# Strided attention: TensorE's program as one loop, values copied by quadrants, the block matrix by 0/1 scales

## Chip, cores and metric

The kernel runs on one core of a Trainium2 chip. The metric is the device time of one execution in microseconds; the time before is the median of three runs.

## The reference

```python
batch, heads, seq, dim = (8, 12, 1024, 64)          # stride = 64, float32
scale = 1.0 / np.sqrt(dim)
attend_positions = np.arange(0, seq, stride)        # the same 16 keys for every query
k, v = K[:, :, attend_positions, :], V[:, :, attend_positions, :]
for i in range(seq):
    scores = np.einsum('bhqd,bhkd->bhqk', Q[:, :, i:i + 1, :], k) * scale
    weights = np.exp(scores - np.max(scores, axis=-1, keepdims=True))
    weights = weights / (np.sum(weights, axis=-1, keepdims=True) + 1e-10)
    result[:, :, i, :] = np.einsum('bhqk,bhkd->bhqd', weights, v)[:, :, 0, :]
```

Each of the 96 heads has 1024 queries of 64 numbers, which all attend to the same 16 of its keys and values. Q (25.2 MB) is read and the result (25.2 MB) written once; of K and V 0.4 MB each are used.

## The kernel before

The work is cut into NG = 24 groups of four heads (HG). For each group g, in order:

- `load(g)` (L232): SP issues a DMA of 1 MB of Q into one of 11 buffers `qn`.
- `cast(g)` (L319): POOL turns it to bf16 (`qb`); for the first three groups ACT takes half.
- `transpose(g)` (L331): DVE transposes it within blocks of 32 into `qt`.
- `score_products(g, k)` (L343): 16 matmuls on TensorE with the group's block of `k_t`, which holds the keys of all groups; the scores land in `sc`.
- `largest` (L361), `raise_` (L371), `sums` (L376), `weights` (L383): softmax over 16 keys. DVE takes the maximum, subtracts it, adds up and inverts; ACT takes the exponential; POOL multiplies by the inverse into `wt`.
- `turn_products(g)` (L392): four transpositions on TensorE bring the weights' keys to the partitions (`tp`).
- `spread(g)` (L404): two ACT copies put `tp` into `wb`, one for each half of the partitions, into the columns of that half alone. The rest of `wb` stays zero from a memset, so that `wb` is block diagonal.
- `output_products(g, n)` (L410): eight matmuls of `wb` with the group's value matrix `v_all`, in two halves n, into `o`.
- `evict(g, n)` (L427): ACT copies each half of `o` to one of eight buffers `out_sb`; it waits for the store of eight groups before.
- `queue(g)` and `store` (L489, L452): SP issues the store of two groups (2 MB) and further loads. SP works its list in order, so a store that waits for its data holds up the loads behind it.

The values need preparation. `value_rows(n)` (L294) has TensorE multiply all values with a permutation matrix `perm_v` (built by POOL from the identity) to repeat their rows where the groups need them, and ACT copies the products to `v_rep`. `values(g)` (L311) then has POOL multiply a group's rows with a 0/1 `mask`, into one of two tiles `v_all`.

`Program` (L43) records operations with what they read and write, and derives the semaphore waits. The order of work of each engine is the order of recording: a prologue (L458 to L479), then for each step i the stages of `ORDER` (L526), each with its lag, so that "turn3" at step i is the turn of group i - 3. Operations of TensorE that are marked `looped` are not written out: `pe_stream` (L532) writes one loop of two groups a turn, with waits on four counters (`turned`, `weighted`, `free0`, `free1`), which it lowers again at each turn's end. `scores(0)`, `scores(1)` and the value products come ahead of that loop, written out: 36 matmuls. The loop has (NG + 2) / 2 = 13 turns, and past the last group its stages run on data that nobody uses. For ACT, DVE and POOL all instructions are written out.

Of the kernel before, what the change touches and what calls it, by code (L numbers as in the profile page):

```python
# [168 lines left out]
def kernel(  # L169
# [32 lines left out]
    k_raw = sb.tile([P, NC, D], FP32, name="k_raw")  # L202
# [3 lines left out]
    k_bf = sb.tile([P, NC, D], BF16, name="k_bf")  # L206
    k_r = sb.tile([P, NC, D], BF16, name="k_r")
    v_bf = sb.tile([P, NC, D], BF16, name="v_bf")
    v_rep = sb.tile([P, NC, 2, D], BF16, name="v_rep")
    identity = sb.tile([P, P], BF16, name="identity")  # L210
    perm_v = sb.tile([P, 2, 2, 2, 2, NK], BF16, name="perm_v")
    s_sel = sb.tile([P, 4], BF16, name="s_sel")
    mask = sb.tile([P, 4, D], BF16, name="mask")
    k_t = sb.tile([P, NG + 4, 2, 4 * NK], BF16, name="k_t")
    v_all = [sb.tile([P, 4, D], BF16, name=f"v_all{i}") for i in range(2)]
# [5 lines left out]
    wt = [sb.tile([P, 32, NK], BF16, name=f"wt{i}") for i in range(2)]  # L221
# [34 lines left out]
    id_v = identity.rearrange("p (c b a k) -> p c b a k", c=2, b=2, a=2)  # L256
    for c in range(2):
        for a in range(2):
            op("POOL", lambda c=c, a=a: nc.gpsimd.tensor_copy(
                out=perm_v[:, c, a],  # L260
                in_=id_v[:, c, :, a].unsqueeze(1).to_broadcast([P, 2, 2, NK]),
            ), reads=["identity"], writes=[f"perm{c}{a}"])
    op("POOL", lambda: nc.gpsimd.memset(k_t, 0.0),  # L263
       writes=[f"k_t{c}{s}" for c in range(2) for s in range(4)])
# [8 lines left out]
    op("POOL", lambda: nc.gpsimd.memset(wb_all, 0.0),  # L273
       writes=[f"wb{i}{a}" for i in range(2) for a in range(2)])
# [8 lines left out]
    def keys(c, h, engine):  # L283
        src, dst = 32 * (2 * c + h // 2), 32 * h
        col = 32 * (h % 2) + NK * (h // 2)
        fn = {"DVE": nc.vector.tensor_copy, "ACT": nc.scalar.copy}[engine]
        op(engine, lambda: fn(  # L287
            k_t[dst : dst + 32, c : NG : 2, :, col : col + NK],
            k_r[src : src + 32].rearrange(
                "p n (a k f) -> p a n f k", a=2, f=2  # L290
            )[:, h % 2],
        ), reads=["k_r"], writes=[f"k_t{c}{h}"])

    def value_rows(n):  # L294
# [12 lines left out]
        op("ACT", lambda: nc.scalar.copy(  # L307
            v_rep[:, 6 * n : 6 * n + 6].rearrange("p n c d -> p c n d"), rows
        ), reads=[f"o{n}"], writes=[f"v_rep{n}"])

    def values(g):  # L311
        op("POOL", lambda: nc.gpsimd.tensor_tensor(  # L312
            out=v_all[g % 2], in0=mask,
            in1=v_rep[:, g // 2, g % 2].unsqueeze(1).to_broadcast([P, 4, D]), op=ALU.mult,
        ), reads=["mask", f"v_rep{g // 12}"], writes=[f"v{g % 2}"])
# [3 lines left out]
    def cast(g, shared):  # L319
# [6 lines left out]
        else:  # L326
            op("POOL", lambda: nc.gpsimd.tensor_copy(out=b, in_=q),  # L327
               reads=[f"qn{g % QBUFS}{h}" for h in range(2)],
               writes=[f"qb{g % 2}{h}" for h in range(2)])

# [12 lines left out]
    def score_products(g, k):  # L343
        for i in range(8):
            for f in range(2):
                r = nc.tensor.matmul(  # L346
                    _ap_with(
                        sc_ps[g % 2], [sc_ps[g % 2].ap[0], [64, 2], [1, 32]],
                        extra_offset=128 * (i // 2) + 32 * (i % 2),
                    ),  # L350
# [5 lines left out]
    def scores(g, looped):  # L356
        op("PE", None if looped else lambda: score_products(g, g),
           reads=[f"qt{g % 2}"] + [f"k_t{g % 2}{h}" for h in range(4)],
           writes=[f"sc{g % 2}"], gates=[("turned", g + 1)], looped=looped)
# [23 lines left out]
    def weights(g):  # L383
# [6 lines left out]
        ), reads=[f"ex{g % 2}", f"rec{g % 2}"], writes=[f"wt{g % 2}"], gate="weighted")  # L390
# [9 lines left out]
    def turn(g, looped):  # L400
        op("PE", None if looped else lambda: turn_products(g),
           reads=[f"wt{g % 2}", "identity"], writes=[f"tp{g % 2}{a}" for a in range(2)], gates=[("weighted", g + 1)], looped=looped)

    def spread(g):  # L404
        for a in range(2):
            rows = slice(64 * a, 64 * a + 64)
            op("ACT", lambda rows=rows: nc.scalar.copy(wb[g % 2][rows, :, rows], tp_ps[g % 2][rows]),  # L407
               reads=[f"tp{g % 2}{a}"], writes=[f"wb{g % 2}{a}"])

    def output_products(g, n):  # L410
# [177 lines left out]
```

## Time and profile before

| what | value |
|---|---|
| median of three runs | 128.34 us (128.32 to 128.53) |
| the profiled execution's own time | 129.04 us |
| its span, first to last instruction | 127.3 us |
| DMA: data moved, mean rate over the span | 51.18 MB, 402 GB/s |
| busiest compute engine | ACT, 96.3 us (76%) |
| TensorE's granted clock, mean | 0.844 |

The times of the profile are microseconds from the span's start. PE is TensorE's matmul, PEld its weight load; DVE, ACT, POOL and SP are VectorE, ScalarE, GpSimd and SyncE. A row of a group of instructions names line, engine, operation, written and read tiles, shapes and count, then the busy time in us, the mean of one in ns, and the idle time before them with what ended it. A row by stage gives from and to in us, the stage's length, the busy time of each compute engine, TensorE's granted clock, the mean busy share of the 16 DMA engines, and the GB/s moved. The rate in a short stage counts a packet where it starts, so shares can pass 1. A row of a DMA queue gives its packets, its MB and the time they took as a share of 16 engines over the stretch asked for.

### The profile page before, as it was taken

How to read it: one execution, taken by the hardware profiler on the slowest of the kernel's cores; microseconds unless marked ns; L12 is line 12 of the kernel's file. 1: busy time of each engine (PE TensorE's matmuls, PEld its weight loads, DVE VectorE, ACT ScalarE, POOL GpSimd, SP SyncE). 2: the span in 40 equal slices, each digit the busy share in tenths (PEclk: the TensorE clock that was granted, in tenths of full speed). 3: DMA queues.
4: the chain of work that ended last, by engine and by line, in shares of the span. 5: the costliest groups of instructions: out<-in, count | busy, mean ns of one | idle time of the engine just before them, and what ended most of it. 6: DMA issues, size and time to landing. Idle time of an engine off the chain costs nothing. (4 is left out here: it accounts for less than half of the span.)

```text
span 127.3 us, 2174 instructions
## 1 busy us (share of the span) xinstructions
PE 66.8 (52%) x764; PEld 47.6 (37%) x764; DVE 83.3 (65%) x126; ACT 96.3 (76%) x136; POOL 88.9 (70%) x88
## 2 busy tenths in 40 slices
PE   0003385684656766575555584274666765595000
PEld 0002353562434544352433372262454544383000
DVE  0105977999999999999999995893794665000000
ACT  4299763599999999999999976965974999983000
POOL 5993388999999999999998992893895344400000
PEclk9999999599997799999999958975555699959555
DMA  2998999989999998998999999999999999999980
GB/s 53 408 422 371 484 391 433 474 366 474 422 402 371 448 469 361 427 469 376 443 448 391 417 469 397 422 453 407 404 438 435 412 422 427 438 412 438 402 363 28
DMA packets 6134, 51.18 MB, mean 402 GB/s; under 512 B 3696, under 2 KB 3696, under 8 KB 3696
## 3 DMA queue, kind: packets, MB, share of 16 engines
q1 hardware_dynamic: 6128, 51.12, 96.2%
q14 instruction: 5, 0.04, 0.1%
q8 instruction: 1, 0.02, 0.0%
HBM read 25.95 MB, written 25.17 MB: 402 GB/s over the span
## 5 line engine op out<-in xcount | busy, mean ns | idle before, releaser
L432 ACT COPY out_sb<-o 128x1024 f32<-128x1024 f32 x48 | 46.4, 1015 | 8.3 <-DMA out_dram<-out_sb 6.1
L327 POOL CAST qb<-qn 128x2048 bf16<-128x2048 f32 x21 | 39.7, 1892 | 6.0 <-DMA qn<-in_Q_dram 6.0
L413 PE MATMUL o<-v_all,wb_all 128*128 128x256 bf16 x208 | 36.3, 318 | 3.0 <-ACT out_sb L432 2.9
L346 PE MATMUL sc<-k_t,qt 128*128 (+1 forms) x448 | 24.0, 213 | 20.2 <-DVE qt L338 15.4
L338 DVE STREAM_TRANSPOSE qt<-qb 128x1024 int32<-128x1024 int32 x24 | 29.7, 1239 | 5.0 <-ACT qb L322 3.6
L387 POOL TENSOR_TENSOR wt<-ex,rec 128x512 bf16<-128x512 f32 x24 | 25.4, 1060 | 9.3 <-DVE rec L380 8.6
L346 PEld LDWEIGHTS sc<-k_t,qt 128*128 128x128 bf16 x448 | 21.1, 111 | 26.6 <-DVE qt L338 13.9
L407 ACT COPY wb_all<-tp 64x512 bf16<-64x512 bf16 x48 | 27.7, 577 | 1.4 <-PE tp L394 1.0
L394 PE MATMUL tp<-identity,wt 128*128 128x128 bf16 x104 | 11.9, 246 | 26.4 <-POOL wt L387 26.4
L413 PEld LDWEIGHTS o<-v_all,wb_all 128*128 128x128 bf16 x208 | 20.5, 112 | 12.1 <-ACT out_sb L432 7.7
L377 DVE TENSOR_REDUCE total<-ex 128x32 f32<-128x512 f32 x24 | 16.3, 681 | 11.0 <-ACT ex L372 9.6
L372 ACT ACTIVATE ex<-low 128x512 f32<-128x512 f32 x24 | 15.4, 642 | 4.5 <-DVE low L367 4.5
L394 PEld LDWEIGHTS tp<-identity,wt 128*128 128x128 bf16 x104 | 6.9, 108 | 29.3 <-POOL wt L387 29.3
L367 DVE TENSOR_TENSOR low<-sc,top 128x512 f32<-128x512 f32 x24 | 16.6, 692 | 0.8
L312 POOL TENSOR_TENSOR v_all<-mask,v_rep 128x256 bf16<-128x256 bf16 x24 | 16.1, 670 | 0.5 <-ACT v_rep L307 0.5
L364 DVE TENSOR_REDUCE top<-sc 128x32 f32<-128x512 f32 x24 | 15.2, 632 | 1.1 <-PE sc L346 1.1
L380 DVE RECIPROCAL rec<-total 128x32 f32<-128x32 f32 x24 | 8.5, 353 | 0.8
L324 POOL CAST qb<-qn 128x1024 bf16<-128x1024 f32 x3 | 3.1, 1041 | 3.6 <-DMA qn<-in_Q_dram 3.6
L287 ACT COPY k_t<-k_r 32x384 bf16<-32x384 bf16 x8 | 4.1, 509 | 0.7 <-DVE k_r L278 0.6
L322 ACT CAST qb<-qn 128x1024 bf16<-128x1024 f32 x3 | 3.1, 1045 | 0.0
L263 POOL MEMSET k_t<- 128x3584 bf16 x1 | 3.1, 3085 | 0.0
L278 DVE STREAM_TRANSPOSE k_r<-k_bf 128x384 int32<-128x384 int32 x1 | 0.6, 579 | 3.5 <-ACT k_bf L277 3.5
(19 smaller groups left out, 11.2 us busy)
## 6 DMA issues: line engine op xcount, KB each, us to landing
qn<-in_Q_dram SPq DMA_DIRECT2D x24, 1024.0 KB, 21.4
out_dram<-out_sb SPq DMA_DIRECT2D x11, 2048.0 KB, 21.5
out_dram<-out_sb SPq DMA_DIRECT2D x2, 1024.0 KB, 10.3
k_raw<-in_K_dram SPq DMA_DIRECT2D x1, 384.0 KB, 4.1
v_raw<-in_V_dram SPq DMA_DIRECT2D x1, 384.0 KB, 6.6
```

The costliest lines, as they stand in the source:

```text
L312: op("POOL", lambda: nc.gpsimd.tensor_tensor(out=v_all[g % 2], in0=mask, in1=v_rep[:, g // 2, g % 2].unsqueeze(1).to_broadcast([P, 4, D]), ...
L327: op("POOL", lambda: nc.gpsimd.tensor_copy(out=b, in_=q), reads=[f"qn{g % QBUFS}{h}" for h in range(2)], writes=[f"qb{g % 2}{h}" for h in ...
L338: op("DVE", lambda: nc.vector.transpose(_ap_with(words, [words.ap[0], [1, 2], [D, 16], [2, 32]]), qb[g % 2].bitcast(I32),), reads=[f"qb{g ...
L346: r = nc.tensor.matmul(_ap_with(sc_ps[g % 2], [sc_ps[g % 2].ap[0], [64, 2], [1, 32]], extra_offset=128 * (i // 2) + 32 * (i % 2),), lhsT=_ ...
L367: op("DVE", lambda: nc.vector.tensor_tensor(out=low, in0=s, in1=m.unsqueeze(2).to_broadcast([P, 32, NK]), op=ALU.subtract,), reads=[f"sc{g ...
L372: op("ACT", lambda: nc.scalar.activation(out=ex[g % 2], in_=low, func=AF.Exp, bias=0.0, scale=scale,), reads=["low"], writes=[f"ex{g % 2}"])
L377: op("DVE", lambda: nc.vector.tensor_reduce(out=total[g % 2], in_=ex[g % 2], op=ALU.add, axis=mybir.AxisListType.X,), reads=[f"ex{g % 2}"] ...
L387: op("POOL", lambda: nc.gpsimd.tensor_tensor(out=wt[g % 2], in0=ex[g % 2], in1=rec[g % 2].unsqueeze(2).to_broadcast([P, 32, NK]), op=ALU.mult,
L394: r = nc.tensor.transpose(tp_ps[g % 2][:, 2 * c : 2 * c + 2].rearrange("p a b -> p (a b)"), wt[g % 2][:, 8 * c : 8 * c + 8].rearrange("p t ...
L407: op("ACT", lambda rows=rows: nc.scalar.copy(wb[g % 2][rows, :, rows], tp_ps[g % 2][rows]), reads=[f"tp{g % 2}{a}"], writes=[f"wb{g % 2}{a}"])
L413: r = nc.tensor.matmul(_ap_with(o_ps, [o_ps.ap[0], [128, 2], [256, 2], [1, D]], extra_offset=512 * c + D * u,), lhsT=wb[g % 2][:, 2 * c + ...
L432: op("ACT", lambda: nc.scalar.copy(to[:, half], o_ps[:, half].rearrange("p c (b x) -> p c b x", b=2)), reads=[f"o{n}"] + ready, writes=[f" ...
```

## The change

TensorE's written-out products go. The loop begins with the first scores and has 14 turns; in its first two steps the stages after the scores run on zeros (`idle`), for which `pe_stream` raises three counters beforehand and three tiles are set to zero. The matmuls of the scores write 64 adjacent columns, since the keys' columns in `k_t` now follow the order of the heads.

The values are no longer permuted by TensorE, repeated or masked. One tile `v_all` holds the value matrices of all groups; POOL sets it to zero and copies blocks of 32 partitions of `v_raw` into it, 24 copies spread over the first steps, by `VALUES`: eight for groups 0 to 3 at step 2, then two a step for four steps and one a step for eight. Each copy is recorded as reading what the POOL operation before it wrote (`apart`).

The block matrix `wb` is written by two ACT activations of all 128 partitions, each with a scale of 0 or 1 for each partition (`sel`), in place of two copies of 64 partitions. The memsets of `k_t` and `wb_all` move from POOL to DVE. The keys' raw tiles share memory with the last output buffer.

```diff
-    k_raw = sb.tile([P, NC, D], FP32, name="k_raw")
+    late = out_all[-1].rearrange("p n b x d -> p (n b x d)")
+    k_raw = late[:, 0 : NC * D].rearrange("p (n d) -> p n d", d=D)
+    k_half = late[:, NC * D : 2 * NC * D].bitcast(BF16).rearrange("p (a n d) -> p a n d", a=2, d=D)
+    k_bf, k_r = [k_half[:, i] for i in range(2)]
...
-    k_bf = sb.tile([P, NC, D], BF16, name="k_bf")
-    k_r = sb.tile([P, NC, D], BF16, name="k_r")
-    v_bf = sb.tile([P, NC, D], BF16, name="v_bf")
-    v_rep = sb.tile([P, NC, 2, D], BF16, name="v_rep")
...
-    perm_v = sb.tile([P, 2, 2, 2, 2, NK], BF16, name="perm_v")
-    s_sel = sb.tile([P, 4], BF16, name="s_sel")
-    mask = sb.tile([P, 4, D], BF16, name="mask")
+    sel = sb.tile([P, 2], FP32, name="sel")
...
-    v_all = [sb.tile([P, 4, D], BF16, name=f"v_all{i}") for i in range(2)]
+    v_all = sb.tile([P, NG + 4, 4, D], BF16, name="v_all")
...
-    wt = [sb.tile([P, 32, NK], BF16, name=f"wt{i}") for i in range(2)]
+    wt_all = sb.tile([P, 2, 32, NK], BF16, name="wt_all")
+    wt = [wt_all[:, i] for i in range(2)]
...
-    id_v = identity.rearrange("p (c b a k) -> p c b a k", c=2, b=2, a=2)
-    for c in range(2):
-        for a in range(2):
-            op("POOL", lambda c=c, a=a: nc.gpsimd.tensor_copy(
-                out=perm_v[:, c, a],
-                in_=id_v[:, c, :, a].unsqueeze(1).to_broadcast([P, 2, 2, NK]),
-            ), reads=["identity"], writes=[f"perm{c}{a}"])
-    op("POOL", lambda: nc.gpsimd.memset(k_t, 0.0),
+    op("DVE", lambda: nc.vector.memset(k_t, 0.0),
        writes=[f"k_t{c}{s}" for c in range(2) for s in range(4)])
-    op("POOL", lambda: nc.gpsimd.memset(v_all[1], 0.0), writes=["v1"])
+    op("DVE", lambda: nc.vector.memset(wt_all, 0.0), writes=["wt0", "wt1"])
+    op("DVE", lambda: nc.vector.memset(wb_all, 0.0),
+       writes=[f"wb{i}{a}" for i in range(2) for a in range(2)])
     op("DVE", lambda: nc.vector.tensor_reduce(
-        out=s_sel, in_=identity.rearrange("p (h s k) -> p s h k", h=2, s=4),
+        out=sel, in_=identity.rearrange("p (q h k) -> p h q k", h=2, k=NK),
         op=ALU.max, axis=mybir.AxisListType.XY,
-    ), reads=["identity"], writes=["s_sel"])
-    op("POOL", lambda: nc.gpsimd.tensor_copy(
-        out=mask, in_=s_sel.unsqueeze(2).to_broadcast([P, 4, D])
-    ), reads=["s_sel"], writes=["mask"])
-    op("POOL", lambda: nc.gpsimd.memset(wb_all, 0.0),
-       writes=[f"wb{i}{a}" for i in range(2) for a in range(2)])
+    ), reads=["identity"], writes=["sel"])
+    op("POOL", lambda: nc.gpsimd.memset(v_all, 0.0),
+       writes=[f"v{c}{a}{b}{m}" for c in range(2) for a in range(2) for b in range(2) for m in range(3)] + ["none"])
...
-        col = 32 * (h % 2) + NK * (h // 2)
+        col = NK * h
...
-    def value_rows(n):
-        rows = o_ps[:, 2 * n : 2 * n + 2, 0 : NC // 2 * D].rearrange("p c (n d) -> p c n d", d=D)
-
-        def products():
-            for c in range(2):
-                r = nc.tensor.matmul(
-                    rows[:, c], lhsT=perm_v[:, c].rearrange("p a i b k -> p (a i b k)"),
-                    rhs=v_bf[:, 6 * n : 6 * n + 6], start=True, stop=True,
-                )
-            return r
-
-        op("PE", products, reads=["v_bf"] + [f"perm{c}{a}" for c in range(2) for a in range(2)],
-           writes=[f"o{n}"])
-        op("ACT", lambda: nc.scalar.copy(
-            v_rep[:, 6 * n : 6 * n + 6].rearrange("p n c d -> p c n d"), rows
-        ), reads=[f"o{n}"], writes=[f"v_rep{n}"])
-
-    def values(g):
-        op("POOL", lambda: nc.gpsimd.tensor_tensor(
-            out=v_all[g % 2], in0=mask,
-            in1=v_rep[:, g // 2, g % 2].unsqueeze(1).to_broadcast([P, 4, D]), op=ALU.mult,
-        ), reads=["mask", f"v_rep{g // 12}"], writes=[f"v{g % 2}"])
+    parts = (slice(0, 2), slice(2, 7), slice(7, NC))
+
+    apart = []
+
+    def values(c, a, b, m):
+        src, dst, part = 32 * (2 * c + b), 32 * (2 * a + b), parts[m]
+        op("POOL", lambda: nc.gpsimd.tensor_copy(
+            out=v_all[dst : dst + 32, 3 + c + 2 * part.start : 3 + c + 2 * part.stop - 1 : 2, 2 * a + b],
+            in_=v_raw[src : src + 32, part],
+        ), reads=["v_raw"] + apart, writes=[f"v{c}{a}{b}{m}"])
+        apart[:] = [f"v{c}{a}{b}{m}"]
...
-               reads=[f"qn{g % QBUFS}{h}" for h in range(2)],
+               reads=[f"qn{g % QBUFS}{h}" for h in range(2)] + apart,
                writes=[f"qb{g % 2}{h}" for h in range(2)])
+            apart[:] = [f"qb{g % 2}0"]
...
-                    _ap_with(
-                        sc_ps[g % 2], [sc_ps[g % 2].ap[0], [64, 2], [1, 32]],
-                        extra_offset=128 * (i // 2) + 32 * (i % 2),
-                    ),
+                    sc_ps[g % 2][:, 64 * i : 64 * i + 64],
...
-        ), reads=[f"ex{g % 2}", f"rec{g % 2}"], writes=[f"wt{g % 2}"], gate="weighted")
+        ), reads=[f"ex{g % 2}", f"rec{g % 2}"] + [k for k in apart if k[0] == "v"], writes=[f"wt{g % 2}"], gate="weighted")
...
-    def turn(g, looped):
-        op("PE", None if looped else lambda: turn_products(g),
-           reads=[f"wt{g % 2}", "identity"], writes=[f"tp{g % 2}{a}" for a in range(2)], gates=[("weighted", g + 1)], looped=looped)
+    def turn(g):
+        op("PE", None, reads=[f"wt{g % 2}", "identity"], writes=[f"tp{g % 2}"],
+           gates=[("weighted", g + 1)] if g >= 0 else [], looped=True)
...
-            rows = slice(64 * a, 64 * a + 64)
-            op("ACT", lambda rows=rows: nc.scalar.copy(wb[g % 2][rows, :, rows], tp_ps[g % 2][rows]),
-               reads=[f"tp{g % 2}{a}"], writes=[f"wb{g % 2}{a}"])
-
-    def output_products(g, n):
+            op("ACT", lambda a=a: nc.scalar.activation(
+                out=wb[g % 2][:, :, 64 * a : 64 * a + 64], in_=tp_ps[g % 2],
+                func=AF.Copy, scale=sel[:, a : a + 1],
+            ), reads=[f"tp{g % 2}", "sel"], writes=[f"wb{g % 2}{a}"])
+
+    def output_products(g, k, n):
...
-                    rhs=v_all[g % 2].rearrange("p s d -> p (s d)"), start=True, stop=True,
+                    rhs=v_all[:, k].rearrange("p s d -> p (s d)"), start=True, stop=True,
...
-        op("PE", None, reads=[f"wb{g % 2}0", f"wb{g % 2}1", f"v{g % 2}"], writes=[f"o{n}"],
-           gates=[(f"free{n}", g + 2)], looped=True)
+        op("PE", None, reads=[f"wb{g % 2}0", f"wb{g % 2}1"] + [
+               f"v{g % 2}{a}{b}{int(g >= 4) + int(g >= 14)}" if 0 <= g < NG else "none" for a in range(2) for b in range(2)
+           ], writes=[f"o{n}"], gates=[(f"free{n}", g + 1)] if g >= 0 else [], looped=True)
...
-        ), reads=[f"o{n}"] + ready, writes=[f"out{g % OBUFS}.{n}"],
+        ), reads=[f"o{n}"] + ready, writes=[f"out{g % OBUFS}.{n}"] + ["k_raw", "k_bf", "k_r"] * (g == OBUFS - RUN and not n),
...
+    def idle(i):
+        scores(i)
+        turn(i - 2)
+        for n in range(2):
+            outputs(i - 3, n)
+
...
-    scores(0, False)
     cast(1, True)
+    idle(0)
     largest(0)
     raise_(0)
     transpose(1)
-    scores(1, False)
-    op("ACT", lambda: nc.scalar.copy(v_bf, v_raw), reads=["v_raw"], writes=["v_bf"])
+    idle(1)
     cast(2, True)
     sums(0)
     weights(0)
-    value_rows(0)
-    values(0)
-    value_rows(1)
-    for n in range(2):
-        free([f"v_rep{n}"], n)
...
+    quadrants = [[(c, a, b, m) for c in range(2) for a in range(2) for b in range(2)] for m in range(3)]
+    VALUES = {0: quadrants[0]}
+    VALUES.update((i + 1, quadrants[1][2 * i : 2 * i + 2]) for i in range(4))
+    VALUES.update((i + 5, quadrants[2][i : i + 1]) for i in range(8))
...
-    turns = (NG + 2) // TURN
+    turns = (NG + 4) // TURN
...
+        elif stage == "values" and g in VALUES:
+            for q in VALUES[g]:
+                values(*q)
...
-    ORDER = "transpose0 cast-1 turn3 spread3 sums2 outA4 largest1 evA4 outB4 evB4 values3 scores0 weights2 raise_1 queue4".split()
+    stages = dict(sums=sums, largest=largest, raise_=raise_, queue=queue)
+    ORDER = "transpose0 cast-1 values2 turn3 spread3 sums2 outA4 largest1 evA4 outB4 evB4 scores0 weights2 raise_1 queue4".split()
...
+        pe.sem_inc(gates["weighted"], 2)
+        for n in range(2):
+            pe.sem_inc(gates[f"free{n}"], 3)
         with pe.Fori(0, turns) as turn_:
             for j in range(TURN):
-                pe.wait_ge(gates["turned"], j + 3)
-                score_products(j, turn_ * TURN + (j + 2)).then_inc(done, 1)
+                i = turn_ * TURN + j
+                pe.wait_ge(gates["turned"], j + 1)
+                score_products(j, i).then_inc(done, 1)
                 pe.wait_ge(gates["weighted"], j + 1)
                 turn_products(j).then_inc(done, 1)
                 for n in range(2):
                     pe.wait_ge(gates[f"free{n}"], j + 1)
-                    output_products(j + 1, n).then_inc(done, 1)
+                    output_products(j + 1, i, n).then_inc(done, 1)
```

More of the change, by code (lines that the diff above doesn't have):

```diff
@@ L354, in score_products, with scores @@
         return r
[L356 to L359, printed above, removed]
+    def scores(g):
+        op("PE", None, reads=[f"qt{g % 2}"] + [f"k_t{g % 2}{h}" for h in range(4)],
+           writes=[f"sc{g % 2}"], gates=[("turned", g + 1)], looped=True)
     def largest(g):
@@ L474 @@
     weights(0)
-    value_rows(0)
-    values(0)
-    value_rows(1)
-    for n in range(2):
-        free([f"v_rep{n}"], n)
     early = dict(
         cast=(0, 1, 2), transpose=(0, 1), scores=(0, 1), largest=(0,), raise_=(0,), sums=(0,),
-        weights=(0,), values=(0,),
+        weights=(0,),
     )
+    quadrants = [[(c, a, b, m) for c in range(2) for a in range(2) for b in range(2)] for m in range(3)]
+    VALUES = {0: quadrants[0]}
+    VALUES.update((i + 1, quadrants[1][2 * i : 2 * i + 2]) for i in range(4))
+    VALUES.update((i + 5, quadrants[2][i : i + 1]) for i in range(8))
     DEPTH = 4
-    turns = (NG + 2) // TURN
+    turns = (NG + 4) // TURN
     ahead = 1
@@ L505, in at @@
         elif stage == "scores" and 0 <= g < NG + 4:
-            scores(g, True)
+            scores(g)
         elif stage == "weights" and 0 <= g < NG + 2:
@@ L509, in at @@
         elif stage == "turn" and 0 <= g < NG + 2:
-            turn(g, True)
+            turn(g)
         elif stage in ("outA", "outB") and -1 <= g < NG + 1:
@@ L516, in at @@
             n = int(stage == "evB")
-            free([f"o{n}"] + ["wb00", "wb01"] * (1 - n), n)
+            free(["wb00", "wb01"], n)
         elif stage in ("evA", "evB") and 0 <= g < NG:
@@ L521, in at @@
             cast(g, False)
+        elif stage == "values" and g in VALUES:
+            for q in VALUES[g]:
+                values(*q)
         elif 0 <= g < NG and stage in stages:
             stages[stage](g)
-    stages = dict(sums=sums, largest=largest, raise_=raise_, queue=queue, values=values)
-    ORDER = "transpose0 cast-1 turn3 spread3 sums2 outA4 largest1 evA4 outB4 evB4 values3 scores0 weights2 raise_1 queue4".split()
+    stages = dict(sums=sums, largest=largest, raise_=raise_, queue=queue)
+    ORDER = "transpose0 cast-1 values2 turn3 spread3 sums2 outA4 largest1 evA4 outB4 evB4 scores0 weights2 raise_1 queue4".split()
     for i in range(1, NG + 5):
```

## The prediction

> **What bounds the kernel now.** I read the page first, for the share of each engine and of the DMA.
>
> ```profile
> span 127.3 us, 2174 instructions
> ...
> PE 66.8 (52%) x764; PEld 47.6 (37%) x764; DVE 83.3 (65%) x126; ACT 96.3 (76%) x136; POOL 88.9 (70%) x88
> ...
> DMA  2998999989999998998999999999999999999980
> ...
> q1 hardware_dynamic: 6128, 51.12, 96.2%
> q14 instruction: 5, 0.04, 0.1%
> q8 instruction: 1, 0.02, 0.0%
> ```
>
> No compute engine is busy for more than 76% of the span, while the 16 DMA engines are busy for 96.2% of it with the data queue alone. The chain of waits follows instructions alone; it ends with TensorE's last matmuls, before the last transfer lands, and does not help here. I asked for busy time by stage instead.
>
> ```profile
> core 0: us, PE busy (x) PEld busy (x) DVE busy (x) ACT busy (x) POOL busy (x), PEclk, DMA share, GB/s
> 39.00:40.00 1.00, 0.62 (x12) 0.59 (x13) 0.96 (x3) 0.90 (x3) 0.93 (x3) 0.83 0.35 147
> 40.00:94.00 54.00, 32.44 (x378) 22.81 (x376) 47.29 (x69) 47.88 (x69) 47.42 (x41) 0.85 1.00 425
> 115.00:123.00 8.00, 1.30 (x13) 0.69 (x10) 0.00 (x0) 0.62 (x1) 0.00 (x0) 0.70 0.99 417
> 123.00:124.00 1.00, 0.00 (x0) 0.00 (x0) 0.00 (x0) 0.00 (x0) 0.00 (x0) 0.50 0.53 221
> 124.00:125.00 1.00, 0.00 (x0) 0.00 (x0) 0.00 (x0) 0.00 (x0) 0.00 (x0) 0.50 0.20 82
> 125.00:126.00 1.00, 0.00 (x0) 0.00 (x0) 0.00 (x0) 0.00 (x0) 0.00 (x0) 0.50 0.08 33
> ...
> 125.00:125.25 0.25, 0.00 (x0) 0.00 (x0) 0.00 (x0) 0.00 (x0) 0.00 (x0) 0.50 0.16 66
> 125.25:125.50 0.25, 0.00 (x0) 0.00 (x0) 0.00 (x0) 0.00 (x0) 0.00 (x0) 0.50 0.08 33
> 125.50:125.75 0.25, 0.00 (x0) 0.00 (x0) 0.00 (x0) 0.00 (x0) 0.00 (x0) 0.50 0.08 33
> ```
>
> By the slices of the page and the DMA share of the stages (next to last column) the queue is full from the third microsecond to 123 us, near 1.00; compute starts, idles and ends under it. So a shorter computation buys nothing, and a slower one costs nothing while the queue stays full. What is left is the tail: at 123 us the rate falls from 417 to 221, then 82, then 33 GB/s. All 16 engines give 425, so one gives 26.6. After 124 us two or three work, after 125.25 us one alone. The kernel waits for its slowest DMA engine, about 2 us after most of the others (123.5 to 125.6).
>
> Why is one late? The page lists six packets that are not data but instructions, one of them on a queue of its own (q8). I narrowed the DMA view until it held that packet: the stretch from 27.5 to 29 us.
>
> ```profile
> q8 instruction: 1, 0.02, 4.2%
> ```
>
> 4.2% of 16 engines in 1.5 us is 1.0 us of one engine (0.042 x 16 x 1.5). An engine that never runs dry cannot make that up: 1.0 us of foreign work at 28 us is still there at 125 us. The trace doesn't name the engine, nor whose instructions these are; that it is the engine that ends last is my reading, since 1.0 us is half of its lateness and no other packet is near that size (the five on q14 hold 0.04 MB together).
>
> **The change part by part.** *TensorE's program.* The 32 score matmuls and 4 value matmuls ahead of the loop go; the loop takes 14 turns in place of 13 and runs 784 matmuls (56 x 14) against 764 and a few lost records. Each matmul has a weight load, so the written program loses 72 of its some 210 instructions. I expect the late instruction block to go with them: TensorE is the engine whose program shrinks by a third, and the packet comes early in the loop's second turn.
>
> ```profile
> 18.76 1.25 PE L413 MATMUL o<-v_all,wb_all 128*128 128x256 bf16 x8
> ...
> 25.44 0.89 PE L346 MATMUL sc<-k_t,qt 128*128 x16
> ```
>
> The second turn's scores begin at 25.44 us, the packet lies 2 us later, and the code past the unlooped part is what has been reached for the first time. [...]
>
> Price: at most 1.0 us by the packet's row, if nobody else were late; below, the next engine decides. From 125.00 to 125.25 two packets of 8 KB start (66 GB/s x 0.25 us = 16 KB), later one per quarter, the last at 125.50 to 125.75. So the second-latest engine starts its last packet some 0.5 us (0.25 to 0.75) before the latest. I take **-0.6 us**, nearer to the second engine's distance than to the packet's 1.0, as it limits first. The other bound is 0: no other row shortens the data. The two passes of the loop that compute nothing yet (outputs of 1.25 us by the row above, turns of half as many matmuls) run while TensorE waits for the second group's queries; if that cover were gone, the second scores would start up to 2 us late, well under the slack that the first store has (below).
>
> *Values and memsets.* POOL loses 24 multiplies, four permutation copies and two memsets; it gains one larger memset and 24 quadrant copies (8 of 128, 16 of 320 elements a partition), each behind a wait for the one before.
>
> ```profile
> L327 POOL CAST qb<-qn 128x2048 bf16<-128x2048 f32 x21 | 39.7, 1892 | 6.0 <-DMA qn<-in_Q_dram 6.0
> L387 POOL TENSOR_TENSOR wt<-ex,rec 128x512 bf16<-128x512 f32 x24 | 25.4, 1060 | 9.3 <-DVE rec L380 8.6
> L312 POOL TENSOR_TENSOR v_all<-mask,v_rep 128x256 bf16<-128x256 bf16 x24 | 16.1, 670 | 0.5 <-ACT v_rep L307 0.5
> L263 POOL MEMSET k_t<- 128x3584 bf16 x1 | 3.1, 3085 | 0.0
> L273 POOL MEMSET wb_all<- 128x2048 bf16 x1 | 1.8, 1805 | 0.0
> L259 POOL COPY perm_v<-identity 128x64 bf16<-128x64 bf16 x4 | 0.8, 238 | 0.1
> ...
> L252 POOL TENSOR_SCALAR_AFFINE_SELECT identity<-identity 128x128 bf16<-128x128 bf16 x1 | 0.3, 295 | 0.2 <-POOL identity L251 0.2
> ```
>
> The memset of 7168 elements is 6.2 us (3085/3584 x 7168), about as long as what goes from the same place (3.1 + 1.8 + 0.8 and two smaller ones). So the first cast begins where it did. A cast costs 0.92 ns an element, so a small copy 0.12 + 0.1 = 0.22 us and a larger 0.40; a wait for the engine's own last result 0.24 us (the 0.2 of L252). Bounds: 0.24 (the 64-element copy) to 0.67 (the multiply). The eight first copies take 8 x (0.22 + 0.24) = 3.7 us in place of one multiply of 0.67 and stand ahead of the cast of group 4 and the weights of group 1: POOL is some 3 us late there. Then come two copies a group for four groups: 1.89 + 1.06 + 2 x 0.64 + 0.24 = 4.5 us against 3.62 now. Who waits: the weights, TensorE, ACT's evictions, and behind them on SP the first store and the loads after it.
>
> ```profile
> 31.45 0.63 SPq L34 DMA_DIRECT2D out_dram<-out_sb  x1
> ...
> 116.78 0.54 SPq L34 DMA_DIRECT2D out_dram<-out_sb  x1
> ...
> out_dram<-out_sb SPq DMA_DIRECT2D x1, 1024.0 KB, 9.7
> ```
>
> The first store is issued at 31.45 us, but its bytes move only when the loads before it are through, at the dip at 39 to 40 us (0.35 above): some 6 us of cover after an issue's lead of 1 to 2. Three microseconds late costs **0**. After that a pair of groups needs 4 MB of DMA, 10 us, against 9 us of POOL at its worst, so the cover grows.
>
> *Block matrix by scales.* Two ACT instructions a group stay, of 128 instead of 64 partitions and the same 512 elements each, now activations with a scale.
>
> ```profile
> L407 ACT COPY wb_all<-tp 64x512 bf16<-64x512 bf16 x48 | 27.7, 577 | 1.4 <-PE tp L394 1.0
> L372 ACT ACTIVATE ex<-low 128x512 f32<-128x512 f32 x24 | 15.4, 642 | 4.5 <-DVE low L367 4.5
> L432 ACT COPY out_sb<-o 128x1024 f32<-128x1024 f32 x48 | 46.4, 1015 | 8.3 <-DMA out_dram<-out_sb 6.1
> ```
>
> Between 577 ns and the 642 of the activation: 0 to 0.13 us a group, 0.8 us over the last six groups. ACT waits for stores in between (6.1 us), so earlier lateness is absorbed. [...] Cost 0. The three memsets on DVE (3328 words) take 3.5 to 5 us at 1 to 1.5 ns a word, ready by 5 to 6.5 us; at worst the keys are 0.5 us late, under the same cover.
>
> **Sum** against the profiled execution: its own time 129.04 us is 1.7 over its span; the median of the runs is 128.34. 129.04 - 0.6 = 128.4 profiled, and 128.34 - 0.6 = **127.7 us** for the median.
>
> **Rivals.** *(1) The block is fetched all the same,* by the loop's back branch or because it is another engine's, or it is not the engine that ends last: 128.3 us. For it: the trace names no owner, and the loop branches back before and after. Against: one packet in 13 turns, so branches alone don't bring it. *(2) The first store comes too late.* It decides if the eight copies and what follows cost over 6 us more than now: from 0.9 us a copy, wait included, over twice my estimate. Then every microsecond beyond is lost: at 1.1 us a copy it is 8 x 1.1 - 0.7 = 8.1, 2 us over, and 128.34 - 0.6 + 2 = 129.7 us. Against: no POOL row of that size costs it. *(3) Another engine gets a block instead.* POOL's written program grows by 15 instructions, semaphore waits above all; a packet of 8 KB at the small blocks' price of 0.3 us (the rate of one engine, 26.6 GB/s) falls on one DMA engine. On the one that ends last, with the old block still there: 128.65 us.
>
> **How the numbers follow.** Forecast (block gone, 127.0 to 128.0) 0.60; rival 1 0.22; rival 2 0.07; rival 3 0.11. The range leaves out rival 2 and a gain beyond all of the packet: 126.9 to 128.65; the forecast's own is 126.9 to 128.0. Its low end is 1.4 us of gain: the last engine is done at some 125.6 us, all but three at some 124.2 (82 GB/s is three engines), and the other late ones may be freed too, since the smaller blocks change as well. Some 0.2% (0.26 us) is what a measurement tells from no change. Faster: 0.60 and a little of rival 1, 0.62; same 0.20; slower 0.18.
>
> **What would show it.** No q8 packet between the start and 60 us, a rate that falls from 400 GB/s to nothing within 2 us, and a span near 126.7: right. A q8 packet that is there still, or the same 2.5 us of tail without it: the step on the block is wrong. A DMA share well under 0.9 for over a microsecond around 35 to 45 us: rival 2. POOL's copies should show 0.2 and 0.4 us, the scaled activations 0.58 to 0.65, the first store 32 to 36 us.

## The result, and the profile after

The changed kernel takes 129.05 us (median of 15 runs, 128.28 to 129.53), the kernel before 128.53 us beside it (15 runs, 128.32 to 128.70): ratio 1.0038, 95% interval 1.0022 to 1.0054. It is slower by some 0.5 us, where 0.6 us of gain was forecast.

The page of the changed kernel, the same lines as before:

```profile
span 127.1 us, 2269 instructions
...
PE 67.3 (53%) x784; PEld 49.9 (39%) x784; DVE 86.2 (68%) x129; ACT 97.0 (76%) x133; POOL 83.3 (66%) x81
...
DMA  1999999999898999999999999999999999999990
...
q1 hardware_dynamic: 6128, 51.12, 96.1%
q14 instruction: 5, 0.04, 0.1%
```

The line of q8 is missing: the packet of 16 KB that the kernel before has there (1638 GB/s over the 10 ns from 27.69 us, in which it is the only packet) is gone, as forecast. DMA is as full as it was (96.1% in q1 against 96.2%), and the span 0.2 us shorter in this one execution. Now the end by stages (from, to, length, the engines' busy times, granted clock, DMA share, GB/s):

```profile
123.00:124.00 1.00, 0.00 (x0) 0.00 (x0) 0.00 (x0) 0.00 (x0) 0.00 (x0) 0.50 0.67 279
124.00:125.00 1.00, 0.00 (x0) 0.00 (x0) 0.00 (x0) 0.00 (x0) 0.00 (x0) 0.50 0.14 57
125.00:126.00 1.00, 0.00 (x0) 0.00 (x0) 0.00 (x0) 0.00 (x0) 0.00 (x0) 0.50 0.04 16
...
125.25:125.50 0.25, 0.00 (x0) 0.00 (x0) 0.00 (x0) 0.00 (x0) 0.00 (x0) 0.50 0.00 0
125.50:125.75 0.25, 0.00 (x0) 0.00 (x0) 0.00 (x0) 0.00 (x0) 0.00 (x0) 0.50 0.08 33
```

Less is left after 124 us (57 and 16 GB/s against 82 and 33), so fewer engines are late in this execution; a second profile of the same kernel (e1) has 131 and 16. And one engine still starts its last packet of 8 KB between 125.50 and 125.75 us, as late as in the kernel before. The tail did not grow shorter.

The span is not the whole time. Each run gives its time and its span; the rest lies before the first and after the last instruction. For the changed kernel it is 2.05 us (median of 15), and for the kernel before 1.77 us (35 runs beside the first experiments). The DMA view of the changed kernel, asked for 127 to 130 us, past the span's end:

```profile
DMA packets 1, 0.01 MB, mean 3 GB/s; under 512 B 0, under 2 KB 0, under 8 KB 0
...
q14 instruction: 1, 0.01, 1.1%
```

One packet of instructions of 8 KB comes there (109 GB/s in one slice of 0.075 us), some 1.6 us after the span's end; the same stretch of the kernel before has no packet at all. This is the second half of the answer: some 0.28 us are lost outside the span. The other 0.24 us of this first comparison stay unexplained: the spans of the kernel before are not on record here, and the repetition below (e1) finds 0.26 us outside the span and 0.05 in it.

What was costed at nothing, in the groups of the changed kernel (line, engine, operation, tiles, shapes, count, busy us, mean ns of one, idle time before) and in SP's list (the changed kernel's first two stores):

```profile
L290 POOL CAST v_all<-v_raw 32x320 bf16<-32x320 f32 x16 | 7.2, 447 | 1.0
L263 POOL MEMSET v_all<- 128x7168 bf16 x1 | 6.1, 6072 | 0.0
...
L290 POOL CAST v_all<-v_raw 32x128 bf16<-32x128 f32 x8 | 2.3, 287 | 0.5
```

```profile
L382 ACT ACTIVATE wb_all<-tp,sel 128x512 bf16<-128x512 bf16 x48 | 30.4, 692 | 4.7 <-PE tp L370 4.5
```

```profile
34.28 0.63 SPq L34 DMA_DIRECT2D out_dram<-out_sb  x1
...
42.40 0.59 SPq L34 DMA_DIRECT2D out_dram<-out_sb  x1
```

The copies take 0.29 and 0.45 us, the memset 6.1. The activations take 692 ns each, above the forecast's 642, but overlap (30.4 us / 48 = 0.63 apart). The first store is issued 2.8 us later (34.28 against 31.45). None of it shows in the DMA line.

### The profile page after: what moved, and what is told of

Its sections match the earlier page's. It is cut to its first block, busy times and chain, and to the rows that moved or that the text cites. A ratio compares the mean times of both kernels' runs of the same rounds, so it can differ in the third digit from the quotient of the medians.

```text
span 127.1 us, 2269 instructions
## 1 busy us (share of the span) xinstructions
PE 67.3 (53%) x784; PEld 49.9 (39%) x784; DVE 86.2 (68%) x129; ACT 97.0 (76%) x133; POOL 83.3 (66%) x81
## 3 DMA queue, kind: packets, MB, share of 16 engines
q1 hardware_dynamic: 6128, 51.12, 96.1%
## 5 line engine op out<-in xcount | busy, mean ns | idle before, releaser
L390 PE MATMUL o<-v_all,wb_all 128*128 x224 | 38.6, 317 | 2.5 <-ACT out_sb L410 0.9
L363 POOL TENSOR_TENSOR wt_all<-ex,rec 128x512 bf16<-128x512 f32 x24 | 25.4, 1057 | 17.6 <-DVE rec L356 16.3
L382 ACT ACTIVATE wb_all<-tp,sel 128x512 bf16<-128x512 bf16 x48 | 30.4, 692 | 4.7 <-PE tp L370 4.5
L326 PE MATMUL sc<-k_t,qt 128*128 x448 | 24.0, 213 | 15.8 <-DVE qt L318 11.9
L370 PE MATMUL tp<-identity,wt_all 128*128 128x128 bf16 x112 | 13.0, 249 | 29.8 <-POOL wt_all L363 28.1
L390 PEld LDWEIGHTS o<-v_all,wb_all 128*128 128x128 bf16 x224 | 22.9, 113 | 10.9 <-ACT out_sb L410 3.9
L370 PEld LDWEIGHTS tp<-identity,wt_all 128*128 128x128 bf16 x112 | 7.6, 109 | 32.8 <-POOL wt_all L363 31.0
L290 POOL CAST v_all<-v_raw 32x320 bf16<-32x320 f32 (+1 forms) x24 | 9.5, 394 | 1.5
L263 POOL MEMSET v_all<- 128x7168 bf16 x1 | 6.1, 6072 | 0.0
L277 ACT COPY k_t<-out_sb 32x384 bf16<-32x384 bf16 x8 | 4.1, 508 | 0.7 <-DVE out_sb L268 0.6
```

Of the source, the lines that this page charges most:

```text
L326: r = nc.tensor.matmul(sc_ps[g % 2][:, 64 * i : 64 * i + 64], lhsT=_ap_with(qt[g % 2], [qt[g % 2].ap[0], [2, P]], extra_offset=2 * P * i + f),
L363: op("POOL", lambda: nc.gpsimd.tensor_tensor(out=wt[g % 2], in0=ex[g % 2], in1=rec[g % 2].unsqueeze(2).to_broadcast([P, 32, NK]), op=ALU.mult,
L370: r = nc.tensor.transpose(tp_ps[g % 2][:, 2 * c : 2 * c + 2].rearrange("p a b -> p (a b)"), wt[g % 2][:, 8 * c : 8 * c + 8].rearrange("p t ...
L382: op("ACT", lambda a=a: nc.scalar.activation(out=wb[g % 2][:, :, 64 * a : 64 * a + 64], in_=tp_ps[g % 2], func=AF.Copy, scale=sel[:, a : a ...
L390: r = nc.tensor.matmul(_ap_with(o_ps, [o_ps.ap[0], [128, 2], [256, 2], [1, D]], extra_offset=512 * c + D * u,), lhsT=wb[g % 2][:, 2 * c + ...
```

## The experiments

All were timed in several rounds, each beside the kernel before on the same chip. There were four series, on four chips: e1 to e4, e5 to e8, e9 to e11, and e12. The kernel before had a median span of 127.10, 127.10, 127.05 and 127.00 us in them, so medians of different series can be set side by side to about 0.1 us. Each of e1 to e12 ran 12 times (e10 six times). The table gives the median time, the median span and the median of time less span, in us; POOL and TensorE are the instructions written in their programs, a matmul with its weight load counted as two.

| kernel | TensorE | POOL | time | span | over the span | ratio to before (95%) |
|---|---|---|---|---|---|---|
| before (with e1 to e4) | 209 | 124 | 128.87 | 127.10 | 1.77 | |
| e1 changed, again | 142 | 139 | 129.17 | 127.15 | 2.03 | 1.0024 (1.0010 to 1.0037) |
| e2 changed, TensorE long | 209 | 139 | 129.19 | 127.15 | 2.03 | 1.0026 (1.0013 to 1.0039) |
| e3 before, POOL long | 209 | 140 | 129.09 | 127.05 | 2.03 | 1.0011 (0.9997 to 1.0026) |
| e4 changed, POOL short | 142 | 106 | 128.79 | 127.00 | 1.78 | 0.9982 (0.9967 to 0.9997) |
| e5 before, POOL 132 | 209 | 132 | 128.94 | 127.15 | 1.81 | 1.0008 (0.9990 to 1.0026) |
| e6 e4, 1 score matmul | 78 | 106 | 128.13 | 126.30 | 1.84 | 0.9940 (0.9921 to 0.9958) |
| e7 e4, stored in reverse | 142 | 106 | 128.71 | 126.90 | 1.79 | 0.9987 (0.9968 to 1.0006) |
| e8 e4 again | 142 | 106 | 128.78 | 127.00 | 1.79 | 0.9992 (0.9975 to 1.0010) |
| e9 e6 + 15 tiny matmuls | 138 | 106 | 128.62 | 126.85 | 1.77 | 0.9990 (0.9979 to 1.0001) |
| e10 e6 + 7 tiny matmuls | 106 | 106 | 128.29 | 126.50 | 1.78 | 0.9962 (0.9948 to 0.9977) |
| e11 e6 + 15 weight loads | 138 | 106 | 128.66 | 126.85 | 1.78 | 0.9995 (0.9979 to 1.0010) |
| e12 e6, TensorE long | 211 | 106 | 128.67 | 126.90 | 1.78 | 0.9981 (0.9961 to 1.0001) |

**e1: the changed kernel once more.**

> The changed kernel once more, unchanged, beside the runs of before on the same chip: a second profile of it and the measure for the other three. Theory A (the gain on the late DMA engine is real, but small, and more is lost outside the span): its executions take 0.2 to 0.3 us longer than their own spans would give before (about 2.0 us over the span against 1.75), the profile again has no q8 packet, and the ratio is 1.002 to 1.006. Rival B (the first result is the spread of this kernel, 128.28 to 129.53, and nothing lasting): ratio 0.998 to 1.002.

It repeats: 0.30 us slower, of which 0.26 (2.03 less 1.77) lie outside the span and 0.05 in it. Rival B falls.

**e2: TensorE's program as long as before.**

```diff
+    def pad_products():
+        for _ in range(33):
+            r = nc.tensor.transpose(
+                tp_ps[0][:, 0:2].rearrange("p a b -> p (a b)"),
+                wt[0][:, 0:8].rearrange("p t k -> p (t k)"), identity,
+            )
+        return r
+    op("PE", pad_products, reads=["wt0", "identity"], writes=["tp0"])
     key_rows()
```

> The changed kernel with 33 written-out transpositions on TensorE ahead of its loop (they read zeros, and their result is overwritten), so that TensorE's program is as long as before (209 instructions against 142). If the length of TensorE's program brings the block of 16 KB, the q8 packet is back and one DMA engine ends 2.0 to 2.4 us after most: the span grows by 0.2 to 0.6 us against the changed kernel. If the packet comes from the loop's branch back or from another engine, there is none here, and the time is that of the changed kernel within 0.2 us.

The packet is back. The DMA view of e2 from 30 to 31.5 us:

```profile
q8 instruction: 1, 0.02, 4.2%
```

So the length of TensorE's program brings the block, as forecast, and not the loop's branch, which both have. But the span does not grow, where 0.2 to 0.6 us were expected: 127.15 us with the block and 127.15 without. The step that failed is the block's price.

**e3 and e5: POOL's program longer, e4: shorter.** e3 adds 16 memsets to the kernel before, e5 adds 8; e4 copies the values of all groups at once.

```diff
+    for n in range(16):
+        op("POOL", lambda n=n: nc.gpsimd.memset(edge[:, n : n + 1], 0.0))
     def pe_stream(sems, gates):
```

> The kernel before with 16 one-column memsets more at the end of POOL's program (a tile that nobody reads), when POOL is done: 140 instructions written in place of 124, as in the changed kernel (139). Theory A, that the longer program of POOL costs a block of instructions after the span: a packet of instructions appears after the span's end, the time over the span goes from 1.75 to 2.0 us, ratio 1.0015 to 1.0025, span the same. Rival: POOL's length does nothing, ratio 0.999 to 1.001.

> The kernel before with 8 one-column memsets more at the end of POOL's program, 132 instructions written in place of 124 (140 brought a block after the span and 2.02 us over it in place of 1.77). [...]

```diff
-    parts = (slice(0, 2), slice(2, 7), slice(7, NC))
+    parts = (slice(0, NC),)
...
     cast(0, True)
+    for q in quadrants[:3]:
+        values(*q)
...
     cast(1, True)
+    for q in quadrants[3:4]:
+        values(*q)
...
-    VALUES = {0: quadrants[0]}
-    VALUES.update((i + 1, quadrants[1][2 * i : 2 * i + 2]) for i in range(4))
-    VALUES.update((i + 5, quadrants[2][i : i + 1]) for i in range(8))
+    VALUES = {0: quadrants[4:]}
```

> The changed kernel with the values copied by 8 copies of all 12 blocks in place of 24, four of them in the prologue: POOL's program has 106 instructions in place of 139. Theory A: no packet of instructions after the span, the time over the span falls back to 1.75 us, and the kernel gains 0.25 us against the changed one: ratio to before 0.999 to 1.003. If the loss lies elsewhere (TensorE's or DVE's program, the slow DMA engine), the time stays that of the changed kernel. The first store may come up to 3 us later than in the changed kernel, without effect.

With 140 instructions the kernel before pays the 0.25 us too (1.77 to 2.03; the ratio's interval still holds 1), with 132 it doesn't (1.81), and the changed kernel with 106 is rid of it (1.78). So POOL's length sets the time over the span; the border lies between 132 and 139 written instructions. The packet past the span tells the same: of all the profiles, the four with 139 or 140 (the changed kernel, e1, e2, e3) have one of 8 KB 1.6 us after the span's end, and no other has any. The view of e4 from 127 to 130 us:

```profile
DMA packets 0, 0.00 MB, mean 0 GB/s; under 512 B 0, under 2 KB 0, under 8 KB 0
```

e4 is also the version that is ahead of the changed kernel (128.79 against 129.17 in the same series) and, by its interval, just ahead of the one before. e8 repeats it:

> e4 unchanged, as the measure for e6 and e7 and a second look at the version that was ahead of both: ratio to before 0.997 to 1.000, about 1.77 us over the span, span 127.0, no block of 16 KB and none after the span.

It is 128.78 us again, 0.08% under the kernel before, with an interval that holds 1.

**Which engine sets the end without the block?** The trace notes when each of the 16 DMA engines has landed its share of a transfer. For the last stores this is how far (us) the latest engine lands behind the median one; for the kernel before and e10 the second-latest is shown too. The trace does not name the engines. The columns are the stores of groups 10-11, 12-13, 14-15, 16-17, 18-19, 20-21, 22 and 23.

```
store               10-11 12-13 14-15 16-17 18-19 20-21   22    23
before, latest       2.36  2.36  2.36  2.36  2.35  2.34  2.37  2.36
before, 2nd latest   0.77  1.00  1.19  1.40  1.65  1.72  1.72  1.77
changed              1.21  1.24  1.49  1.71  2.01  1.99  1.95  1.99
e1, the same         0.50  0.90  0.87  1.06  1.33  1.33  1.32  1.36
e4                   1.31  1.44  1.66  1.90  2.16  2.14  2.11  2.16
e8                   1.26  0.97  0.98  1.19  1.47  1.49  1.47  1.51
e6                   1.07  0.80  0.81  0.81  0.80  0.76  0.77  0.78
e9                   1.15  0.75  0.93  1.13  1.42  1.42  1.40  1.42
e10, latest          1.17  1.09  1.08  1.09  1.16  1.20  1.20  1.23
e10, 2nd latest      0.62  0.65  0.80  0.98  1.08  1.07  1.09  1.10
e12                  2.17  2.16  2.18  2.17  2.17  2.19  2.16  2.18
```

In the kernel before, the latest engine keeps its distance. That it is the one that carries the block shows in the earlier landings: in the transfer that lands next after the q8 packet, the latest engine's distance jumps from 0.38 to 1.80 us (0.25 to 1.87 in e2, 0.14 to 1.78 in e3, 0.31 to 1.44 in e5, 0.54 to 1.52 in e12), and in these five the latest engine stays 0.9 us late or more from there on. The second-latest falls behind by 0.2 us a store, until the computation ends (at 115 us), and then stops. In the changed kernel, e1 and e4 the latest engine falls behind in the same way; I take it for that second one. How far it has come at the end differs by 0.6 us between two profiles of the same kernel (1.99 and 1.36), so the growth from store to store is the safer reading. A steady step with each store is seen only where stores are alone, from 94 us on. Before that, while loads share the queue, the distances wander (0.3 to 0.7 us for the second-latest of the kernel before, from 40 to 92 us), though TensorE works there too. No run explains that difference. Two theories were set against each other: the instructions that run beside the stores, or the stores themselves.

**e6: one score matmul in place of 16. e7: stores to other addresses.** e6, and e9 to e12 which build on it, leave the scores out, and e7 writes the groups to other places of the result; they measure time alone.

```diff
-        for i in range(8):
-            for f in range(2):
-                r = nc.tensor.matmul(
...
-        return r
+        return nc.tensor.matmul(
+            sc_ps[g % 2], lhsT=_ap_with(qt[g % 2], [qt[g % 2].ap[0], [2, P]]),
+            rhs=k_t[:, NG : NG + 4].rearrange("p n f k -> p (n f k)"), start=True, stop=True,
+        )
```

```diff
-            _ap_with(out, [[16 * D, P], [2 * SD, 2 * n], [1, 16 * D]], g * HG * SD),
+            _ap_with(out, [[16 * D, P], [2 * SD, 2 * n], [1, 16 * D]], (NG - n - g) * HG * SD),
```

> The changed kernel with 8 value copies (e4), and the scores of a group made by one matmul of 512 zero columns in place of 16 of 64: the scores are left out, every weight is 1/16. Theory D: in the phase of stores alone one DMA engine falls behind by 0.2 us a store of 2 MB, until the computation ends, because of the instructions that run beside it; TensorE's are most of them, and with 13 matmuls a group in place of 28 the engine falls behind by half as much: the tail after 124 us is shorter, the median span 0.3 to 0.6 us less than e4's 127.0. Rival S: the stores themselves make it (their addresses, or how they are split over the engines), whatever runs beside them: span within 0.15 us of e4's.

> e4, with each store sent to the place of the group as far from the end as its own is from the start, so the same data goes to other addresses (heads end up in other places of the output). Theory D (instructions): one engine still falls behind in the late stores, span within 0.15 us of e4's. Rival S by addresses: the engine that falls behind in the stores of groups 12 to 19 now does so at another time or not at all; the total may be the same, but the landings of the late stores keep their distances from 94 us on.

e7's span is e4's within 0.1 us, and its latest engine falls behind in the same stores (1.37 to 2.08 us from groups 12-13 to 18-19): not the addresses. In e6 nobody falls behind, and the span is 0.7 us shorter. Its end by stages:

```profile
123.00:124.00 1.00, 0.00 (x0) 0.00 (x0) 0.00 (x0) 0.00 (x0) 0.00 (x0) 0.50 0.78 328
124.00:125.00 1.00, 0.00 (x0) 0.00 (x0) 0.00 (x0) 0.00 (x0) 0.00 (x0) 0.50 0.10 41
125.00:126.00 1.00, 0.00 (x0) 0.00 (x0) 0.00 (x0) 0.00 (x0) 0.00 (x0) 0.50 0.00 0
```

No packet starts after 125 us, where the changed kernel had one between 125.50 and 125.75. That TensorE's matmuls were busy no less is seen from 94 to 112 us, first in e8, then in e6:

```profile
94.00:112.00 18.00, 11.47 (x122) 8.25 (x119) 7.98 (x17) 15.22 (x21) 4.27 (x6) 0.72 1.01 429
```

```profile
94.00:112.00 18.00, 11.65 (x57) 6.73 (x58) 7.67 (x17) 15.28 (x21) 3.96 (x6) 0.50 1.01 430
```

The number behind the stage's length is the matmuls' busy time, 11.47 and 11.65 us, with 122 and 57 matmuls: the same time, half the instructions. What else is different in e6 is what the matmuls read, so the next three separate count from data. The granted clock differs too (0.72 and 0.50), but it is 0.54 in this stretch of e9, where the span is long again.

**e9, e10, e11: tiny matmuls, and weight loads, added to e6.**

```diff
+        for _ in range(15):
+            nc.tensor.matmul(
+                sc_ps[g % 2][0:1, 0:1], lhsT=_ap_with(qt[g % 2], [qt[g % 2].ap[0], [2, 1]]),
+                rhs=k_t[:, NG, 0, 0:1], start=True, stop=True,
+            )
         return nc.tensor.matmul(
```

This is e9; e10 has 7 of them. In e11 the 15 have full weights (128 rows of output, `[2, 128]`).

> e6 (the scores left out, one matmul of 512 zero columns) with 15 matmuls of one row and one column ahead of it: as many matmuls a group as the changed kernel has, with next to no data. Theory D1 (it is the number of TensorE's instructions that slows one DMA engine): that engine falls behind again by 0.2 us a store from 94 us on, and the median span is back at 126.8 to 127.1. Theory D2 (it is what the matmuls and weight loads read): no engine falls behind, span 126.2 to 126.5 as in e6.

> The same with 7 tiny matmuls: 20 a group, between e6's 13 and the changed kernel's 28. D1 in proportion: span 126.5 to 126.75, halfway. D1 with a threshold: either end. D2: 126.2 to 126.5.

> The same with 15 matmuls whose weights are full blocks of 128x128 and that move one column: the weight loads of the changed kernel without its moving data. D1: as e9, 126.8 to 127.1. D2: the weight loads read 32 KB each, by far the most that TensorE reads for the scores, so an engine falls behind here and not in e9: span 126.8 to 127.1 here, 126.2 to 126.5 there.

With 13, 20 and 28 matmuls a group the span is 126.30, 126.50 and 126.85 us, and it makes no difference whether the added ones load one column of weights or 128 (126.85 both). The engine that falls behind is back in e9; in e10 it is the second-latest, which comes from 0.65 to 1.08 us between groups 12-13 and 18-19, 0.14 us a store. The number of TensorE's instructions it is, not what they read.

**e12: the block alone.** e6 with 66 transpositions ahead of the loop, written as in e2.

> e6 (the scores left out, one matmul of 512 zero columns a group) with 66 written-out transpositions on TensorE ahead of the loop, so that its written program is as long as before (210 instructions), while the loop stays short. Theory: the block of 16 KB costs its 1.0 us and more on one DMA engine, as forecast, and only the other late engine hid it; with that one no longer late (e6), the block shows. A q8 packet is there, and the span goes from e6's 126.3 to 126.9 to 127.3 us. Rival: the block costs next to nothing even alone: 126.2 to 126.5 us with a q8 packet. Without a q8 packet it tells nothing, and the span is e6's.

The page of e12, and the end by stages:

```profile
q8 instruction: 1, 0.02, 0.0%
```

```profile
124.00:125.00 1.00, 0.00 (x0) 0.00 (x0) 0.00 (x0) 0.00 (x0) 0.00 (x0) 0.50 0.29 123
125.00:126.00 1.00, 0.00 (x0) 0.00 (x0) 0.00 (x0) 0.00 (x0) 0.00 (x0) 0.50 0.08 33
```

The block is there, and the median span goes from 126.30 to 126.90 us: 0.6 us, where the same block cost nothing in e2. The ratios to the kernel before tell the same (0.9940 and 0.9981, with intervals that do not meet). So a block does cost what was forecast where the other engine is not late. That the two figures agree so well is in part luck: the forecast's came from a distance between two engines in one execution of another kernel. And e12's executions spread from 126.3 to 127.3 us; the profiled one is among the longest, and its second-latest engine is 1.65 us late at the end as well, from before 94 us, for a cause that no run here shows.

## Why the prediction was wrong

- *What bounds the kernel:* right. DMA is full from the third microsecond to 123 us (a share of 1.01 from 40 to 94 us and 0.98 from 115 to 123 in the changed kernel), and the slowest DMA engine sets the span (57 GB/s are left after 124 us, and its last packet starts after 125.50). Everything that the change did to POOL, DVE and ACT stayed under it (the dip at 39 to 40 us is no deeper, a DMA share of 0.50 against 0.35); the first store came 2.8 us later, within the forecast 32 to 36 us, and cost nothing. The lead of an issue, put at 1 to 2 us, is 1.1 us at the first load of the kernel before (issued at 0.95 us, first packet at 2.06).
- *The block goes with TensorE's written-out matmuls:* right (no q8 packet in the changed kernel, one in e2 and e12, where the program is long again). That the packet's moment pointed there was luck: at 27.7 us the loop's second turn runs code that the first has run already, and in e2, e3, e5 and e12 the packet starts at 30.5, 35.3, 56.2 and 36.2 us. The runs tie the packet to the length of TensorE's program: it is there with 209 and 211 written instructions (e2, e12), not with 142 (the changed kernel); why that length brings it no run shows. A branch back alone does not: the changed kernel's loop branches back through 14 turns without a q8 packet. Rival 1, that the block is fetched all the same, fell on the cause, though a span as before, which it foretold, is what came.
- *The price, -0.6 us:* here it failed. The step took "the second-latest engine starts its last packet some 0.5 us before the latest" from one execution, as if that distance were the gain of every execution. For that execution the reading was right: the last landings are 0.59 us apart. In the other three profiles of a long TensorE program with all its scores they are 0.27 (e2), 0.14 (e3) and 0.27 us (e5) apart. The prediction's own sign against this step came: the tail to 125.50 us and beyond, without the packet. Where the spans are on record, the median moved by no more than 0.1 us: 127.15 (e1) and 127.00 (e4, e8) against 127.10 for the kernel before beside them. The second engine is late for a reason of its own, 0.2 us a store while TensorE's instructions run (e6 to e11), and ends nearly as late as the one with the block. The 0.6 us are real only where it does not (e12).
- *Nothing outside the span:* the sum carried "1.7 over its span" over unchanged. It grew by 0.26 us (e1; 0.28 in the first comparison), and this is the loss as far as it repeats (0.30 us in e1; the 0.24 us more of the first comparison stay open). Rival 3 had named POOL's longer program and its 8 KB, but had put it on a DMA engine within the span; it comes after the span's end, where the trace shows nothing else that could hide it (e3, e4, e5).
- *Sizes of what lay under cover:* the first eight copies took 0.34 us each with their waits against 0.46; the larger 0.48 against 0.64; the three memsets on DVE 2.95 us (0.89 ns a word) against 3.5 to 5 (DVE's rows in the kernel before have 1.21 ns a word for the transposition L338 and 1.35 for the subtraction L367); the scaled activations 692 ns against at most 642. The zero for these at the last stores was the author's estimate, and no run shows that term by itself; what the changed kernel shows is a DMA share of 1.01 from 94 to 112 us and 0.98 from 115 to 123, against 1.01 and 0.99 in the kernel before. The list of what POOL loses was short by a memset and the copy of `mask`, and the 764 matmuls were all on record (36 + 13 x 56). None of it changed the time.
- *The range* (126.9 to 128.65) missed the median of 129.05 us by 0.4, of which 0.2 is that the kernel before measured 128.53 here and 128.34 in the three runs it was made from. Its low end was wider than its reason: 1.4 us of gain, where all of the packet is 1.0.

What stays open: every run here comes with a recorded span, so it can't be told whether TensorE's instructions or their recording load the one DMA engine. Why the engine falls behind only beside stores alone is open too, and so is what triggers the q8 packet at its moment.

## What to carry to other kernels

Here DMA is full from start to end, the end is the latest of 16 engines, and freeing that one is worth only the distance to the next (0.14 to 0.59 us in four profiles), which may be late for a cause of its own: look at that one, in more than one profile, before pricing a gain. Count the written instructions of every engine on both sides of a change, semaphore waits too, and compare the time less the span: here GpSimd's program, grown from 124 to 139 instructions, was paid with 0.26 us after the last instruction, where nothing covered it. Few long instructions on TensorE in place of many short ones may help a DMA-bound kernel though TensorE's busy time is the same; here it is shown only with the scores left out (e6 against e8, a span of 126.30 against 127.00 us).

## What the runs showed of the hardware

One DMA engine loses time while TensorE issues many instructions beside stores alone: from 13 to 28 matmuls a group (24 groups) the span grows by 0.55 us (126.30 to 126.85), whatever they read, whether by the instructions or by their recording. A block of 16 KB of TensorE's instructions makes one DMA engine 1.0 to 1.6 us later at once (five profiles: the kernel before, e2, e3, e5, e12), and costs 0.6 us of span where no other engine ends as late (e6 and e12). A block of 8 KB of GpSimd's instructions after the span costs 0.25 us (e3, e4). Across all profiles the first transfers landed with up to 0.3 us of difference (the keys' median engine at 4.49 us in the kernel before, at 4.69 in e3, which starts the same), so one profile's start is no evidence for a change there.
